# Block products for the attention's feature-major columns of the long sequence

## The chip, the cores and the metric

The kernel runs on one core of a Trainium2 chip. That core has five engines that run side by side, each with a queue of its own: TensorE (PE, matrix products; its weight loads are shown as PEld), VectorE (DVE), ScalarE (ACT), GpSimd (POOL) and SyncE (SP), which here issues nearly all DMAs. The metric is the time of one execution in microseconds of the device; lower is better.

## The reference

One layer of an encoder is computed for two inputs: a short sequence of 1024 tokens (s = 0) and a long one of 2048 tokens (s = 1), each with 16 learned meta tokens ahead of it. All numbers are fp32.

```python
xn = _rmsnorm(h, g_pre)
proj = xn @ w_in + b_in            # 1024 -> 6672 columns
na_q, na_k, na_v, na_z, ml_qk, ml_v, ml_z, ml_o, ml_g, mg = jnp.split(proj, SPLIT_IDX, axis=-1)
ya = (_neighbourhood_attention(na_q, na_k, na_v, na_rpb) * silu(na_z)) @ w_a
yb = (_mlstm_branch(ml_qk, ml_v, ml_g, ml_o, ml_conv_w, ml_head_g) * silu(ml_z)) @ w_b
ga, gb = split(sigmoid(mg), 2)
y = (ga * ya + gb * yb) @ w_out
return h + _rmsnorm(y, g_post)
```

The attention has 8 heads of 64 features; its queries see a window of 8 x 16 cells of a grid 64 cells wide, and the meta tokens. The mLSTM has 4 heads of 128 features, runs forwards and backwards in chunks, and passes a state from chunk to chunk.

## The kernel before, in words

*Exactness.* The products run on operands of the type F32R. Each fp32 operand is split into a high part and a low part, and each product is three matmuls: high x high, high x low, low x high (mm3, L197 to L202).

*Dense and sparse work.* Two Python generators are interleaved. `sparse` (L1990) is the mLSTM and the attention, in the order mLSTM short, attention short, mLSTM long, attention long. `dense` (L1943) is the large products: the input projection group by group, then the final groups (`final`: the branch projections with the merging by gates, then the output projection). After each sparse step `run` (L2008) takes dense work until its planned cost is used up. The planned cost of a step is `A_N[s]` for the attention (0.94 and 1.085 us), `A_A` and others for the mLSTM. One attention unit (`na`, L1019: one head, one row block of 512 queries, one of four column blocks) has four steps; the long sequence has 4 x 8 x 4 = 128 units and the short one 64. If a sparse stage needs a dense group that isn't done, dense work runs alone until it is. TensorE's instructions stay in the order that this interleaving writes; the other engines' order is set by a scheduler.

*Dense groups.* `PLAN` (L41) lists them as (sequence, first token, columns), each over 1024 tokens, that is two halves of 512. "m" are the mLSTM's columns, "n" the attention's (Q, K and Z feature-major, 12 columns of 128 features; V token-major), "g" the 16 columns of the gates. A feature-major column of a half is 8 depth tiles x 3 = 24 matmuls of 128x512 (`fm_half`, L666), and its result is evacuated by `fm_evac` (L616) from one of three PSUM banks into a staging tile "st" of four buffers and stored to DRAM.

*Block products.* The gates of the long sequence (`sgates`, L880) take the columns in pairs. A pair, the two halves of the tokens and the two halves of the depth make a 2 x 2 block product, which is computed with 7 products of 4 depth tiles instead of 8, from sums and differences of the operands. The weights' combinations are made once by `wprep` (L555) and kept in DRAM (tiles q...); the activations' combinations are made by `tprep` (L586) for each 1024 tokens, beside the group "n" of those tokens, stored, and loaded by `tload` into a pool that takes the place of the pool bp (`gopen`, `gclose`). Where a block group follows another with other tokens, its first two pairs ("lead") are computed in the plain way while the operands of the others are loaded. `beside` (L539) issues these preparations step by step, every few dense yields ("turns").

*Weights.* `requests` (L796) writes down all weight tiles in the order of use. `wpump` (L275) loads each ahead of use into four buffers; a tile seen for the first time is split into its parts, which are stored for later groups. A block unit is the high and low part of one product's weights, 512 KB.

*The attention's inputs.* `na_prep` (L1088) loads one head's raw queries (qr), keys (kr), values (vr) and Z (zt), and splits them into the tiles stk, qB, kd, kx and vt, in six pieces beside the units of the head before.

Of the kernel before, what the change touches and what calls it, by code (L numbers as in the profile page):

```python
# [2 lines left out]

# [6 lines left out]
F32 = mybir.dt.float32  # L10
# [7 lines left out]
P = 128  # L18
TCARGS = dict(schedule_with_timeline_sim=True)
D = 1024  # L20
# [20 lines left out]
PLAN = ((0, 0, "m"), (0, 0, "n"), (1, 0, "m"), (1, 1024, "m"), (1, 1024, "n"), (1, 0, "n"), (1, 0, "g"), (1, 1024, "g"), (0, 0, "g"), ("f", 0, 0), ("f", 0, 1), ("f", 1, 0), ("f", 1, 1), ("f", 1, 2), ("f", 1, 3))  # L41
SW = ((1, 0), (1, 1024))
OPS = ("11", "12", "21", "22", "s1", "s2", "s3", "s4")
# [8 lines left out]
FM_COLS = [c + P * j for c in (C_NQ, C_NK, C_NZ, C_MQ, C_MK, C_MZ) for j in range(4)] + [C_GA + P * j for j in range(16)]  # L52
TM_COLS = [(C_NV, 256), (C_NV + 256, 256), (C_MV, 256), (C_MV + 256, 256), (C_MO, WU), (C_MO + WU, WU)]
# [79 lines left out]
A_N, A_D, A_A, A_G = (0.94, 1.085), 1.63, 1.79, 1.3  # L133


class K:
# [3 lines left out]
    def __init__(self, tc, ins, outs):  # L140
# [10 lines left out]
        self.side, self.qd, self.TD = None, {}, {}  # L151
# [123 lines left out]
    def wpump(self, most=NBW, parts=1, copy=None):  # L275
# [4 lines left out]
        while self.wraw and self.wout < most:  # L280
# [14 lines left out]
            else:  # L295
# [7 lines left out]
                self.wkept[key] = []  # L303
                for x, part in ((hi, "h"), (lo, "l")):
# [152 lines left out]
    def build_half(self, s, t0, res):  # L457
# [14 lines left out]
        if s == 0:  # L472
# [23 lines left out]
            def rows():  # L496
# [4 lines left out]
                self.side, self.pace = self.wprep(), 4  # L501
# [37 lines left out]
    def beside(self):  # L539
# [5 lines left out]
        if self.side and self.turn % self.pace == 0:  # L545
            with self.behind():
                if next(self.side, "end") == "end":
                    self.side = None

    def drain(self):  # L550
        while self.side:
            if next(self.side, "end") == "end":
                self.side = None

    def wprep(self):  # L555
# [6 lines left out]
        for p in range(8):  # L562
            raw = pool.tile([P, 2, 2, 512], F32, name="pr", bufs=1)
            for f in range(2):
                nc.sync.dma_start(raw[:, f].rearrange("p a c -> p (a c)"), self.i["wu"][unit["i", C_GA + (2 * p + f) * P, P], :, :D])
            for _ in range(3):
                yield
            for f, ops in ((0, ("11", "12")), (1, ("21", "22")), (1, ("s3", "s1")), (0, ("s2", "s4"))):
# [14 lines left out]
                yield  # L583
                yield
# [81 lines left out]
    def fm_half(self, col, w, x, s, t0, meta, done=None, tags=None, late=None):  # L666
# [10 lines left out]
        for j, (q, k) in enumerate(order):  # L677
# [3 lines left out]
            wh, wl = (w[k % 2][:, 0, k // 2], w[k % 2][:, 1, k // 2]) if col >= C_GA else (w[0][:, k, :], w[1][:, k, :])  # L681
# [100 lines left out]
    def layout(self, cols):  # L782

        fm = dict(m=[c + P * j for c in (C_MQ, C_MZ, C_MK) for j in range(4)], n=[c + P * j for c in (C_NQ, C_NK, C_NZ) for j in range(4)],
                  g=[C_GA + P * j for j in range(16)])
        tm = dict(m=[(C_MO, WU), (C_MO + WU, WU), (C_MV, 256), (C_MV + 256, 256)],
                  n=[(C_NV, 256), (C_NV + 256, 256)], g=[])
# [4 lines left out]
    def lead(self, j):  # L792

        return [] if PLAN[j - 1][:2] == PLAN[j][:2] else [0, 1]

    def requests(self):  # L796
# [3 lines left out]
        for j, (s, t0, cols) in enumerate(PLAN):  # L800
# [3 lines left out]
            else:  # L804
                keys = []
                for kind, c in self.layout(cols):
                    if j >= 3 and ahead:
                        keys.append(ahead.popleft())
                    if cols == "g":
                        continue  # L810
                    keys += [("i", x, P) for x in c] if kind == "fm" else [("t", *c, a) for a in range(2)]
                if cols == "g":
                    assert not ahead
                    pairs = list(range(8))
# [65 lines left out]
    def sgates(self, s, t0, lead, nxt):  # L880
# [3 lines left out]
        for hf in range(2):  # L884
            if hf == 0:
                ws = [self.wtake(1)[0] for _ in range(2 * len(lead))]
            for u, w in enumerate(ws):
# [4 lines left out]
                yield from self.fm_half(C_GA + (2 * p + f) * P, w, self.xs[hf], s, t0 + 512 * hf, False, done=self.wdone if hf else None)  # L892
        for _ in more:
            pass
        pairs = [p for p in range(8) if p not in lead]
# [31 lines left out]
        for i, p in enumerate(pairs):  # L927
# [8 lines left out]
            out(2 * p, 0, new(), A)  # L936
# [6 lines left out]
            c22, c21 = new(), new()  # L943
            nc.vector.tensor_tensor(c22, E, u7, op=ALU.add)
# [7 lines left out]
            out(2 * p, 1, new(), E)  # L952
            A, E, R = R, A, E
        if nxt:
            self.xs = nx

    def group(self, s, t0, meta, cols, reuse, nxt):
# [3 lines left out]
        nb = None  # L961
        sw = (s, t0) in SW and cols == "n"
        if sw:
            self.drain()
            self.side, self.pace = self.tprep(s, t0), 3
            sw = (s, t0, "g") in PLAN[:PLAN.index((s, t0, "n")) + 2]
        for j, (kind, c) in enumerate(jobs):
# [6 lines left out]
            if last and sw:  # L974
                self.drain()
                self.gopen()
                for _ in self.tload(s, t0, (1, 2, 3)):
                    pass
            ws = self.wtake(len(c))
            for hf in range(2):  # L980
# [16 lines left out]
                for u, (col, w) in enumerate(zip(c, ws)):  # L997
                    for q, cost in enumerate(self.fm_half(col, w, self.xs[hf], *todo[hf], done=self.wdone if hf else None, tags=tags, late=late)):
# [89 lines left out]
    def na_prep(self, np_, s, rows, heads, j):  # L1088
# [6 lines left out]
        qr = np_.tile([P, 512], F32, name="qr", bufs=1)  # L1095
        stk = np_.tile([P, 4, P], F32R, name="stk", bufs=2)
        qb = self.qB[hh]
        nc.sync.dma_start(qr[0:64], self.NQ[s][pr][h0:h0 + 64, rt * 512:(rt + 1) * 512])
        sv = stk.rearrange("p b t -> p (b t)")
# [987 lines left out]
```

## Time and profile before

| | |
|---|---|
| median of the runs | 2732.97 us (2728.5 to 2733.58, 3 runs) |
| profiled execution, its own time | 2734.13 us |
| span in the profile | 2732.4 us |
| TensorE busy | 2691.8 us, 16144 matmuls |
| VectorE busy | 1877.1 us |
| ScalarE busy | 1389.1 us |
| moved by DMA | 762.76 MB |
| mean granted TensorE clock | 0.994 |

A row of a group gives the line, the engine, the operation, output <- inputs with tile shapes and a count; behind the bar the busy time and the mean of one in ns; behind the second bar the engine's idle time just before them, with what ended it. A row of the waits gives who waited <- for whom, the total in us, the number of times and the longest. A row in order of time gives the start and the length in us. A matmul's length overlaps the next one's. A row of a stretch gives its length, then busy time and count of each engine, the granted clock, the share of the DMA engines and GB/s.

### The profile page before, as it was taken

How to read it: one execution, taken by the hardware profiler on the slowest of the kernel's cores; microseconds unless marked ns; L12 is line 12 of the kernel's file. 1: busy time of each engine (PE TensorE's matmuls, PEld its weight loads, DVE VectorE, ACT ScalarE, POOL GpSimd, SP SyncE). 2: the span in 40 equal slices, each digit the busy share in tenths (PEclk: the TensorE clock that was granted, in tenths of full speed). 3: DMA queues.
4: the chain of work that ended last, by engine and by line, in shares of the span. 5: the costliest groups of instructions: out<-in, count | busy, mean ns of one | idle time of the engine just before them, and what ended most of it. 6: DMA issues, size and time to landing. Idle time of an engine off the chain costs nothing.

```text
span 2732.4 us, 47321 instructions
## 1 busy us (share of the span) xinstructions
PE 2691.8 (99%) x16144; PEld 2372.7 (87%) x16144; DVE 1877.1 (69%) x5174; ACT 1389.1 (51%) x3302; POOL 16.7 (1%) x100
## 2 busy tenths in 40 slices
PE   9999999999999999999999999999999999999998
PEld 7998897899789988788898888787888989989898
DVE  5443687876657765569877576573668798897844
ACT  6322556654456554456545564562455656555421
POOL 0000000000000000000000000000000000000000
PEclk9999999999999999999999999999999999999999
DMA  9987888986878755779888889989559898989975
GB/s 372 344 283 280 311 283 313 334 290 236 297 236 281 237 194 192 253 244 346 299 285 301 269 262 380 317 281 296 160 176 312 259 316 263 330 268 296 311 250 207
DMA packets 397538, 762.76 MB, mean 279 GB/s; under 512 B 50192, under 2 KB 179168, under 8 KB 395760
## 3 DMA queue, kind: packets, MB, share of 16 engines
q1 hardware_dynamic: 396176, 757.04, 81.9%
q0 software_dynamic: 1120, 2.69, 0.4%
q8 instruction: 128, 2.10, 0.3%
q14 instruction: 114, 0.93, 0.1%
HBM read 514.89 MB, written 244.69 MB: 278 GB/s over the span
## 4 chain that ended last, share of the span: by engine, by line
PE 87%; DMA 7%; DVE 3%; ACT 2%; issue 1%; SPq 0%; DVEq 0%; ACTq 0%
PE pj L200 14%; PE pj L202 13%; PE pj L201 13%; PE pj L720 5%; PE pj L722 5%; PE pj L721 5%; PE pj L1849 3%; PE pj L1848 3%; PE pj L1850 3%; PE pj L912 3%; PE pj L914 3%; PE pj L913 3%; PE sm L1197 3%; PE tr L1182 3%; DMA va<-mv 1%; DMA whi<-q 1%
## 5 line engine op out<-in xcount | busy, mean ns | idle before, releaser
L200 PE MATMUL pj<-xh,whi 128*128 128x512 f32 (+1 forms) x1376 | 539.3, 392 | 1.6 <-ACT whi L301 1.4
L202 PE MATMUL pj<-xh,wlo 128*128 128x512 f32 (+1 forms) x1376 | 525.4, 382 | 1.1 <-DMA wlo<-wl 0.8
L201 PE MATMUL pj<-xl,whi 128*128 128x512 f32 (+1 forms) x1376 | 525.5, 382 | 0.1
L720 PE MATMUL pj<-whi,xh 128*128 128x256 f32 (+1 forms) x1152 | 330.6, 287 | 0.0
L721 PE MATMUL pj<-wlo,xh 128*128 128x256 f32 (+1 forms) x1152 | 326.1, 283 | 0.0
L722 PE MATMUL pj<-whi,xl 128*128 128x256 f32 (+1 forms) x1152 | 326.1, 283 | 0.0
L202 PEld LDWEIGHTS pj<-xh,wlo 128*128 128x128 f32 x1376 | 259.7, 189 | 54.9 <-DMA wlo<-wl 1.2
L200 PEld LDWEIGHTS pj<-xh,whi 128*128 128x128 f32 x1376 | 260.0, 189 | 44.7 <-ACT whi L301 2.2
L201 PEld LDWEIGHTS pj<-xl,whi 128*128 128x128 f32 x1376 | 260.2, 189 | 41.3 <-issue 1.0
L720 PEld LDWEIGHTS pj<-whi,xh 128*128 128x128 f32 x1152 | 218.7, 190 | 0.4
L721 PEld LDWEIGHTS pj<-wlo,xh 128*128 128x128 f32 x1152 | 218.6, 190 | 0.1
L722 PEld LDWEIGHTS pj<-whi,xl 128*128 128x128 f32 x1152 | 218.4, 190 | 0.0
L1848 PE MATMUL pj<-whi,mh 128*128 128x256 f32 x768 | 216.3, 282 | 0.4 <-DMA whi<-wh 0.4
L1850 PE MATMUL pj<-whi,mlo 128*128 128x256 f32 x768 | 216.0, 281 | 0.0
L1849 PE MATMUL pj<-wlo,mh 128*128 128x256 f32 x768 | 215.9, 281 | 0.0
L1189 DVE TENSOR_TENSOR pts<-tr,pts 96x384 fp32r<-96x384 f32 (+2 forms) x192 | 119.0, 620 | 68.2 <-ACT pts L1184 66.1
L1184 ACT ACTIVATE pts<-tr 96x384 fp32r<-96x384 f32 (+2 forms) x192 | 103.6, 540 | 109.1 <-PE tr L1182 108.1
L200 PE MATMUL pj<-yh,whi 128*128 128x512 f32 x384 | 154.6, 403 | 0.0
L202 PE MATMUL pj<-yh,wlo 128*128 128x512 f32 x384 | 152.0, 396 | 0.0
L201 PE MATMUL pj<-yl,whi 128*128 128x512 f32 x384 | 151.3, 394 | 0.0
L1848 PEld LDWEIGHTS pj<-whi,mh 128*128 128x128 f32 x768 | 144.9, 189 | 1.7 <-DMA whi<-wh 0.6
L1849 PEld LDWEIGHTS pj<-wlo,mh 128*128 128x128 f32 x768 | 144.7, 188 | 1.0
(363 smaller groups left out, 6112.0 us busy)
## 6 DMA issues: line engine op xcount, KB each, us to landing
whi<-wh SPq DMA_DIRECT2D x160, 512.0 KB
wlo<-wl SPq DMA_DIRECT2D x160, 512.0 KB
wraw<-wu SPq DMA_DIRECT2D x48, 512.0 KB
wh<-whi SPq DMA_DIRECT2D x48, 512.0 KB
wl<-wlo SPq DMA_DIRECT2D x48, 512.0 KB
gt<-st SPq DMA_DIRECT2D x96, 256.0 KB
tg<-gt SPq DMA_DIRECT2D x96, 256.0 KB
whi<-q SPq DMA_DIRECT2D x45, 512.0 KB
```

Source lines behind the costliest of these rows:

```text
L200: mm(out, ah, bh, start=start, stop=False)
L201: mm(out, ah, bl, start=False, stop=False)
L202: mm(out, al, bh, start=False, stop=stop)
L720: nc.tensor.matmul(o, xh, wh, start=k == 0, stop=False)
L721: nc.tensor.matmul(o, xh, wl, start=False, stop=False)
L722: nc.tensor.matmul(o, xl, wh, start=False, stop=k == KT - 1)
L912: mm(bank, w[:, 0, k], xh[:, k], start=fresh and k == 0, stop=False, skip_group_check=True)
L1184: nc.scalar.activation(pts[:ks, :nb, 0, :], pt[:ks, :nb], AF.Copy)
L1189: self.nc.vector.tensor_tensor(pts[:ks, :nb, 1, :], pt[:ks, :nb], pts[:ks, :nb, 0, :].bitcast(F32), op=ALU.subtract)
L1848: nc.tensor.matmul(o, mh[:, k, xs], wh, start=clear > 0 and k == 0, stop=False)
L1849: nc.tensor.matmul(o, mh[:, k, xs], wl, start=False, stop=False)
L1850: nc.tensor.matmul(o, ml[:, k, xs], wh, start=False, stop=clear < 2 and k == KT - 1)
```

## The change

For the long sequence the 12 feature-major columns of the attention are computed as block products too. The groups "n" and "g" of the same 1024 tokens become one group "ng" of 14 pairs, and the attention's token-major V columns ("v") move into the mLSTM's groups. `nprep` makes the combined weights of the six new pairs; `wprep` goes on making those of the eight gate pairs. The four plain quarters of a new pair's weights are written when these weights are first split, in the short sequence's group. The activations' combinations are made beside the group "mv" of the tokens. In `sgates` the results go out through `fm_evac`. The pace constants of the attention change. In the attention's pool the raw queries are loaded into stk and the raw keys into kx, where their split parts end up as well, and Z has one buffer, loaded later; that is 8 KB per partition less.

```diff
-PLAN = (... (1, 1024, "m"), (1, 1024, "n"), (1, 0, "n"), (1, 0, "g"), (1, 1024, "g"), (0, 0, "g"), ...)
+PLAN = ((0, 0, "m"), (0, 0, "nv"), (1, 0, "mv"), (1, 1024, "mv"), (1, 1024, "ng"), (1, 0, "ng"), (0, 0, "g"), ...)
-A_N, A_D, A_A, A_G = (0.94, 1.085), 1.63, 1.79, 1.3
+A_N, A_D, A_A, A_G = (1.08, 0.965), 1.63, 1.79, 1.3
+N_COLS = FM_COLS[:12]
+PAIRS = [tuple(c[2 * p:2 * p + 2]) for c in (N_COLS, FM_COLS[24:]) for p in range(len(c) // 2)]
...
 def wpump
+                if key[1] in N_COLS and key[0] == "i":
+                    j = N_COLS.index(key[1])
+                    for a in range(2):
+                        d = self.qd[j // 2, f"{j % 2 + 1}{a + 1}"] = self.dp.tile([P, D], F32, name=f"q{j}{a}")
+                        for h, x in enumerate((hi, lo)):
+                            self.hold.append((d[:, 512 * h:512 * h + 512], x[:, 512 * a:512 * a + 512].bitcast(F32)))
...
-                self.side, self.pace = self.wprep(), 4
+                self.wside = self.wprep()
+                self.sides.append([self.wside, 3])
...
+    def nprep(self):
+        op = lambda o, a, b, x=ALU.subtract: nc.vector.tensor_tensor(o, a, b, op=x)
+        for p in range(6):
+            r0, r1 = [self.bp.tile([P, 2, 512], F32, name="xr", bufs=4) for _ in range(2)]
+            for f, r in enumerate((r0, r1)):
+                nc.sync.dma_start(r.rearrange("p a c -> p (a c)"), self.i["wu"][unit["i", PAIRS[p][f], P], :, :D])
+            for _ in range(2):
+                yield
+            op(r1[:, 1], r1[:, 0], r1[:, 1], ALU.add)
+            op(r1[:, 0], r0[:, 0], r1[:, 0])
+            yield
+            op(r0[:, 0], r1[:, 1], r0[:, 0])
+            op(r0[:, 1], r0[:, 1], r0[:, 0])
+            yield
+            for r, ops in ((r1, ("s3", "s1")), (r0, ("s2", "s4"))):
+                hi = self.bp.tile([P, 2, 512], F32, name="xr", bufs=4)
+                nc.scalar.activation(hi.bitcast(F32R), r, AF.Copy)
+                op(r.bitcast(F32R), r, hi)
+                for q, o in enumerate(ops):
+                    d = self.qd[p, o] = self.dp.tile([P, D], F32, name=f"q{p}{o}")
+                    nc.sync.dma_start(d[:, :512], hi[:, q])
+                    nc.sync.dma_start(d[:, 512:], r[:, q])
+                yield
...
 def sgates
-        def out(c, t, st, x):
-            bi = 36 + c
-            nc.scalar.activation(st, x, AF.Tanh, bias=self.bfh[:, bi:bi + 1], scale=0.5)
-            nc.sync.dma_start(self.GT[s][c][:, t0 + 512 * t:t0 + 512 * t + 512], st)
+        def out(f, t, x):
+            self.fm_evac(PAIRS[p][f], s, t0 + 512 * t, False, [(0, 512)], [x])
...
-            c22, c21 = new(), new()
+            c22 = new()
             nc.vector.tensor_tensor(c22, E, u7, op=ALU.add)
-            out(2 * p + 1, 1, c22, c22)
-            nc.vector.tensor_tensor(c21, A, u7, op=ALU.add)
-            out(2 * p + 1, 0, c21, c21)
+            out(1, 1, c22)
+            nc.vector.tensor_tensor(u7, A, u7, op=ALU.add)
+            out(1, 0, u7)
...
 def group
+        sw = (s, t0) in SW
         if sw:
-            self.drain()
-            self.side, self.pace = self.tprep(s, t0), 3
+            last = t0 > 0
+            self.sides.append([chain(self.tprep(s, t0), self.nprep() if last else ()), 2 if last else 4])
...
+            if last and sw and t0:
                 self.gopen()
-                for _ in self.tload(s, t0, (1, 2, 3)):
-                    pass
+                more = self.tload(s, t0, (1, 2, 3))
...
 def na_prep
-        qr = np_.tile([P, 512], F32, name="qr", bufs=1)
+        qr = sv.bitcast(F32)
-        kr = np_.tile([P, 16, 64], F32, name="kr", bufs=1)
+        kr = kx.bitcast(F32)
...
-            nc.scalar.activation(sv[0:64], qr[0:64], AF.Copy)
+            nc.scalar.activation(qb[0:64], stk[0:64].bitcast(F32), AF.Copy)
         yield
-        nc.scalar.activation(qb[0:64], stk[0:64].bitcast(F32), AF.Copy)
-        nc.vector.tensor_tensor(sv[64:128], qr[0:64], sv[0:64].bitcast(F32), op=ALU.subtract)
+        nc.vector.tensor_tensor(sv[64:128], qr[0:64], qb[0:64].rearrange("p b t -> p (b t)").bitcast(F32), op=ALU.subtract)
+        nc.scalar.activation(sv[0:64], qb[0:64].rearrange("p b t -> p (b t)").bitcast(F32), AF.Copy)
...
+        if hh:
+            zt = np_.tile([P, 512], F32, name="zt", bufs=1)
+            nc.sync.dma_start(zt, self.NZ[s][pr][:, rt * 512:(rt + 1) * 512])
```

More of the change, by code (lines that the diff above doesn't have):

```diff
@@ L2 @@
 from contextlib import ExitStack, contextmanager
+from itertools import chain
 import numpy as np
@@ L544, in beside @@
                 self.nc.sync.dma_start(*self.xput.popleft())
[L545 to L548, printed above, removed]
+        for x in tuple(self.sides):
+            if self.turn % x[1] == 0:
+                with self.behind():
+                    if next(x[0], "end") == "end":
+                        self.sides.remove(x)
     def drain(self):
-        while self.side:
-            if next(self.side, "end") == "end":
-                self.side = None
+        for x in self.sides:
+            for _ in x[0]:
+                pass
+        self.sides = []
     def wprep(self):
@@ L935, in sgates @@
             yield from prod(E, "s2", False)
-            out(2 * p, 0, new(), A)
+            out(0, 0, A)
             yield from prod(R, "s3", True)
@@ L951, in sgates @@
             yield from prod(E, "s4", False)
-            out(2 * p, 1, new(), E)
+            out(0, 1, E)
             A, E, R = R, A, E
+            if p == 5:
+                self.done.add(("n", s, t0))
         if nxt:
```

78 lines of the change are left out of this document (43 added, 35 removed).

## The prediction

> **What bounds the kernel now.** I read the page first, then the groups of instructions by shape, the waits of TensorE and the stretches.
>
> ```profile
> span 2732.4 us, 47321 instructions
> PE 2691.8 (99%) x16144; PEld 2372.7 (87%) x16144; DVE 1877.1 (69%) x5174; ACT 1389.1 (51%) x3302; POOL 16.7 (1%) x100
> DVE  5443687876657765569877576573668798897844
> q1 hardware_dynamic: 396176, 757.04, 81.9%
> PE 87%; DMA 7%; DVE 3%; ACT 2%; issue 1%; SPq 0%; DVEq 0%; ACTq 0%
> ```
>
> TensorE is busy in 99% of the span and makes 87% of the chain that ended last. VectorE reaches eight and nine tenths only in the last quarter. The DMA engines are 82% occupied, so they have no great reserve either. "Busy" can hide slow matmuls, so the next view is the order of time: two runs of back-to-back matmuls, first and last row of each. L200 to L202 are the plain products, L912 to L914 the block products.
>
> ```profile
> 1003.11 0.39 PE L200 MATMUL pj<-xh,whi 128*128 128x512 f32 x1
> ...
> 1004.26 0.39 PE L202 MATMUL pj<-xh,wlo 128*128 128x512 f32 x1
> 1525.44 0.40 PE L912 MATMUL pj<-t3h,wlo 128*128 128x512 f32 x1
> ...
> 1528.00 0.40 PE L914 MATMUL pj<-t3h,wlo 128*128 128x512 f32 x1
> ```
>
> Between the first pair lie 5 starts in 1.15 us, 0.230 us each; between the second 11 starts in 2.56 us, 0.233 us each. A row's 0.39 us overlaps its neighbours and is no price. A 512-wide matmul thus takes 0.231 us of TensorE in either form. Where TensorE does stand still, the waits and the stretches tell (columns of a stretch: length; busy time and count of PE, PEld, DVE, ACT, POOL; granted clock; DMA share; GB/s).
>
> ```profile
> PE tr L1469 <- DVE kf L1433: 6.1, 2, 4.3
> PE sc L1598 <- DVE nwy L160: 6.0, 1, 6.0
> PE pj L912 <- ACT pj L931: 1.3, 2, 0.8
> PE sm L1197 <- ACT prb L1165: 0.7, 2, 0.4
> 450.00:700.00 250.00, 247.14 (x1564) 222.42 (x1565) 186.95 (x590) 136.02 (x347) 0.90 (x8) 0.98 0.84 291
> 770.00:1085.00 315.00, 314.71 (x1992) 283.32 (x1991) 213.68 (x555) 174.34 (x381) 1.81 (x14) 1.00 0.70 231
> 1140.00:1200.00 60.00, 53.85 (x405) 52.41 (x404) 40.15 (x107) 25.74 (x73) 0.31 (x2) 0.91 0.87 284
> 1470.00:1855.00 385.00, 380.19 (x1895) 316.36 (x1894) 254.24 (x854) 216.66 (x574) 1.93 (x10) 1.00 0.92 306
> 1905.00:2600.00 695.00, 693.99 (x4298) 618.63 (x4298) 551.73 (x1366) 381.44 (x898) 2.04 (x4) 1.00 0.84 269
> ```
>
> These are the short sequence's mLSTM (its second half), its attention, the start of the long sequence's mLSTM, the block products of the gates beside that mLSTM, and the long sequence's attention. In the last TensorE loses 1 us of 695. So the time is the count of matmuls times their pitch, plus a few stalls.
>
> **The change part by part.**
>
> *Matmuls.* A pair of columns over 1024 tokens costs 2 columns x 2 halves x 8 depth tiles x 3 = 96 matmuls in the plain form, and 7 products x 4 x 3 = 84 as block products. Before, 16 gate pairs less the 2 that lead the second group, so 14, use the block form; after, 28 pairs less 2, so 26. That is 12 more pairs and 12 x 12 = 144 matmuls fewer, 16144 to 16000. At 0.231 us it is 33.3 us. All of it lies on the path, since TensorE has no idle time there to absorb it.
>
> A page of the Trainium skill ("TensorE: Matmul & The Clock Gate", section "Back-to-back issue gap") gives about 131 ns per matmul for a sustained stream of this width; by it the gain would be an estimated 18.9 us. The two runs above contradict it for these operands, and the sum goes by the runs.
>
> *Preparing the weights.* nprep forms the combined weights of six pairs, in work of this kind:
>
> ```profile
> L598 DVE TENSOR_TENSOR xr<-xh,xl 128x1024 f32<-128x1024 f32 x16 | 19.3, 1214 | 1.6 <-DMA va<-mv 1.5
> L600 DVE TENSOR_TENSOR xr<-xr 128x512 f32<-128x512 f32 x8 | 5.5, 686 | 0.6 <-DMA t2l<-xr 0.6
> L609 DVE TENSOR_TENSOR xr<-xr 128x1024 fp32r<-128x1024 f32 x8 | 9.8, 1222 | 13.2 <-ACT xr L608 13.1
> L608 ACT ACTIVATE xr<-xr 128x1024 fp32r<-128x1024 f32 x8 | 8.4, 1051 | 1.1 <-DVE xr L601 1.1
> L944 DVE TENSOR_TENSOR st<-pj,st 128x512 f32<-128x512 f32 x14 | 9.7, 690 | 7.9 <-PE pj L914 6.5 <-issue 1.4
> L938 ACT ACTIVATE pj<-pj 128x512 f32<-128x512 f32 x14 | 8.1, 581 | 8.7 <-PE pj L914 8.7
> ```
>
> Per pair: 4 x 0.686 + 2 x 1.222 = 5.2 us of VectorE and 2 x 1.051 = 2.1 us of ScalarE, so 31 and 13 us in all. It runs beside the short sequence's attention, where VectorE has 315 - 214 = 101 us free. There it meets the activation split of the second 1024 tokens, which moves too (tprep, four rounds of 2 x 1.214 + 6 x 0.686 + 1.222 = 7.8 us, 31 us), leaving some 40 us. The other split moves beside the mLSTM stretch 450 to 700, whose 63 us of free VectorE shrink to about 32. On TensorE this costs nothing while that cover lasts. Without it mLSTM steps wait as in the first two rows of waits: bounds 0 and the 6 us of one such wait per stretch; I take 2 us in all.
>
> *Evacuation.* Each further block pair needs 2 sums like L944 and 3 copies like L938: 12 x 2 x 0.69 = 17 us of VectorE and 12 x 3 x 0.58 = 21 us of ScalarE. Beside the mLSTM (385 us with 254 and 217 busy) both have room. What is on the path is a product waiting for its bank: 1.3 us over 14 pairs. The 12 more pairs give 1.1 us. The results now go through fm_evac, which takes a fresh staging buffer of four for each, and two for the Z columns. The fourth result of a Z pair can then find its buffer still being stored, with ScalarE queueing behind it and mLSTM steps behind ScalarE. No row shows this wait; its bounds are 0 and, for 4 Z pairs, 4 times the 4.3 us wait on kf, 17 us. I take 2 us, nearest to the bank waits. Evacuation: 3 us.
>
> *DMAs and queues.*
>
> ```profile
> DMA packets 397538, 762.76 MB, mean 279 GB/s; under 512 B 50192, under 2 KB 179168, under 8 KB 395760
> whi<-q SPq DMA_DIRECT2D x45, 512.0 KB
> xh<-xh SPq DMA_DIRECT2D x12, 1024.0 KB
> 1153.63 1.22 SPq L779 DMA_DIRECT2D nv<-stT  x2
> ```
>
> A block pair streams 3.5 MB of weights where a plain pair streams 2. By the order of the two programs, 84 more 512 KB loads of block operands and 48 fewer plain loads add 19 MB, nprep's loads and stores 19 MB. One fewer change of token group saves 8 loads of 1 MB and 32 stores of 256 KB, 17 MB. Net about 21 MB of 763, so 82% becomes about 85%. The block stage already ran at share 0.92, and the block products' largest wait there is the one on a bank, hence 0; without that cover the net 21 MB cost 21/763 of the span, 75 us, in waits. SP issues 80 more DMAs; at 0.6 us each that is 48 us spread over the span, ahead of weight loads that run four buffers ahead.
>
> *Moved work.* The V columns of the attention go into the earlier groups, and so do both splits. The long mLSTM's first head (1140 to 1200) therefore loses its neighbours: the V stores, 0.6 us of SP each, that stood ahead of its loads. That stretch lost 6.2 us to idling, and at clock 0.91 up to 5.4 us more to half rate. Block products now stand there, and they have waits of their own (4.8 us in 385). Bounds: minus 11.6 and 0; I take minus 5.
>
> *The attention's pool.* The raw query and key land in the tiles that hold the split operands, and the Z tile is single and loaded late. Instruction counts per head stay. The new wait is ScalarE's third copy behind VectorE's difference; queued behind it are the exponentials and the copies of transposed probabilities. Between them and TensorE stands a whole unit, 695/128 = 5.4 us. Bounds: 0, and the 0.4 us wait on prb once for each of 32 heads, 13 us; the value is taken with the next item.
>
> *Pace.* The planner's dense work per attention step falls from 1.085 to 0.965 us in the long sequence (128 units of 4 steps, 61 us less) and rises from 0.94 to 1.08 in the short (64 units, 36 us more). So the long attention packs into about 695 - 61 = 634 us. VectorE decides whether it can. Here are two stretches of gate merging, with attention beside and without, and the one VectorE row that counts the units:
>
> ```profile
> 2308.00:2364.00 56.00, 55.70 (x308) 47.60 (x308) 52.44 (x123) 27.95 (x61) 0.00 (x0) 1.00 1.05 342
> 2644.00:2688.00 44.00, 44.00 (x232) 37.59 (x231) 23.97 (x36) 4.90 (x9) 0.00 (x0) 1.00 0.96 353
> L1189 DVE TENSOR_TENSOR pts<-tr,pts 128x512 fp32r<-128x512 f32 (+1 forms) x10 | 6.3, 629 | 0.9 <-ACT pts L1184 0.8
> ```
>
> The 10 units in the first cost 52.4 - 24.0 = 28.5 us of VectorE, 2.85 each, and 56 - 44 = 12 us of TensorE, 1.2 each. By TensorE's order the five such stages hold 57 units after, where 50 stood, so 11.4 each: 24.0 + 11.4 x 2.85 = 56.5 us of VectorE against 44 + 11.4 x 1.2 = 57.7 of TensorE, 98% where 94% stood. VectorE idled 3.6 us in the first row; if it must idle as long again, a stage needs 60.1 us, 2.4 more than TensorE. The DMA share there is full already, but the bytes of a stage grow no faster than its length. Bounds for both items: 0, and 5 x 2.4 + 13 = 25 us. I take 5 us, one us a stage, nearest to the waits of 1 us that the stretch has now.
>
> *The sum.* 2734.1 (the profiled execution) - 33.3 + 2 + 3 - 5 + 5 = 2705.8 us. The median of the runs, 2733.0, is 1.1 us below the profiled one, so 2704.7, say 2705.
>
> **The rivals.**
>
> *Slower: the long attention can't run faster.* If VectorE, already at 94% beside gate merging, refuses the new pace, the attention keeps its 695 us, and the 61 us of dense work taken from its side come after it: 2705 - 5 + 61 = 2761. It decides from the point where about half of the shortening fails, 33 us of waits or 6.6 us in each merging stage. Against it: the sum of 98%, and the 1 us of TensorE waits in that stretch now. For it: a reserve of only 1.2 us per stage, and a new ScalarE wait behind VectorE's queue in each head.
>
> *Part of the gain goes in the block stage.* The staging-buffer wait at its bound (17 us rather than 2) and the attention's at its bound (25 rather than 5) would add 35 us and cancel the gain; half of that gives 2722. For it: DMA share 0.92. Against it: ScalarE is little more than half busy there.
>
> *No change.* The removed matmuls would be cover, and the waits of the mLSTM steps show instead. The 33 us would come back as idle time of TensorE, and the time stays at 2733. TensorE's 380 of 385 busy speaks against it.
>
> *More than the matmuls.* All 11.6 us of the first head's stall vanish and no new waits come: 2705 - 6.6 - 10 = 2688. In that row the clock falls with the stall. The Trainium skill's same page, section "Part 1: The HAM clock gate", says that about 3.4 us of idling halves TensorE's clock; this trace agrees (4.3 us of wait, then 0.91).
>
> **How the numbers follow.** Forecast (2695 to 2716) 0.58; more than the matmuls 0.13; part of the gain goes 0.15; no change 0.04; slower 0.10. A difference of 0.2%, 5.5 us, is about what runs of this kernel can tell from none. Faster 0.86, same 0.04, slower 0.10. The range reaches from the best case, 2688, to 2727, which leaves out the worse half of the partial loss and the slower rival.
>
> **What would show it.** PE count 16000 and busy about 2660 us; L912's successors 728 rows per line; VectorE near 1925 us, ScalarE near 1425; about 783 MB. The stretch of the first mLSTM head without kf waits and at clock 1.0. The long attention in about 634 us, merging stages with VectorE above 96% and TensorE waits under 2 us each. I am wrong if TensorE idles more than 15 us over the five merging stages, if ScalarE waits on stores of staging buffers, or if the attention's span stays near 695.

## The result, and the profile after

The changed kernel takes 2704.61 us (median of 4 runs, 2702.04 to 2705.33) against 2733.27 us before: a ratio of 0.9897, 95% interval 0.988 to 0.9914. It is faster by 1.0%; 2705 was forecast. The profiled execution took 2705.3 us with a span of 2703.3, 29.1 us less than the span before. From the page of the changed kernel:

```profile
span 2703.3 us, 47407 instructions
PE 2658.4 (98%) x16000; PEld 2345.6 (87%) x16000; DVE 1910.4 (71%) x5234; ACT 1418.5 (52%) x3350; POOL 17.4 (1%) x100
DMA packets 405986, 783.72 MB, mean 290 GB/s; under 512 B 51472, under 2 KB 180448, under 8 KB 404208
q1 hardware_dynamic: 404624, 778.01, 85.6%
```

TensorE has its 16000 instructions and 2658 us; VectorE grew by 33 us where 48 were counted, ScalarE by 29 where 34 were; the DMAs moved 21 MB more. The next rows are four of the six stages, of the kernel before and then of the changed one: the short mLSTM, the short attention, the long mLSTM and the long attention. Ahead of them lies the start, behind them the rest. The columns are the length, busy time and count of PE, PEld, DVE, ACT and POOL, the granted clock, the DMA share and GB/s.

```profile
267.00:765.00 498.00, 485.69 (x2973) 429.32 (x2972) 368.57 (x1075) 270.88 (x646) 6.74 (x34) 0.99 0.84 293
765.00:1081.00 316.00, 315.71 (x1996) 284.17 (x1995) 214.37 (x555) 175.23 (x381) 1.22 (x6) 1.00 0.70 229
1081.00:1899.00 818.00, 802.30 (x4300) 682.84 (x4299) 560.31 (x1783) 436.43 (x1140) 4.82 (x30) 0.99 0.87 294
1899.00:2604.00 705.00, 703.99 (x4359) 627.54 (x4358) 556.31 (x1378) 385.10 (x907) 2.04 (x4) 1.00 0.84 269
```

```profile
267.00:778.00 511.00, 494.46 (x3189) 445.71 (x3188) 391.76 (x1101) 269.71 (x641) 7.58 (x34) 0.98 0.88 305
778.00:1135.00 357.00, 352.24 (x2330) 320.66 (x2328) 272.32 (x655) 200.09 (x416) 1.23 (x6) 1.00 0.85 287
1135.00:1934.00 799.00, 796.20 (x3941) 663.05 (x3940) 524.02 (x1728) 450.02 (x1173) 4.64 (x30) 1.00 0.86 285
1934.00:2589.00 655.00, 647.88 (x4167) 583.94 (x4166) 541.73 (x1368) 377.89 (x904) 2.05 (x4) 1.00 0.87 276
```

Two things stand out. The long mLSTM idles 2.8 us where it idled 15.7, and the short mLSTM idles 16.5 where it idled 12.3. Idle time misses what half a clock costs, so for the comparison I use one number per stage, the *loss*: for each two neighbouring instructions of TensorE, the time from start to start less the median of that time for the same two shapes in the profile before, summed over the stage.

| loss in us | start | short mLSTM | short attention | long mLSTM | long attention | rest | sum |
|---|---|---|---|---|---|---|---|
| before | 8.0 | 24.5 | 9.8 | 31.5 | 12.7 | 1.2 | 87.8 |
| after | 9.9 | 35.0 | 11.9 | 10.5 | 21.1 | 2.4 | 90.8 |

Without loss the two orders differ by 32.3 us; with 3.0 us more loss, 29.3 are left, and the spans differ by 29.1. The sum of the losses hardly moved, but those of single stages did. Each loss is of one execution. How far it scatters shows in the long attention, whose code is the same in the changed kernel and in six of the variants below: there it lies between 17.5 and 21.4 us.

The five longest waits of TensorE in the changed kernel, and behind them that on the block product's bank:

```profile
PE sm L1247 <- ACT prb L1215: 4.7, 8, 1.3
PE sm L1200 <- DVE yg L1262: 4.5, 4, 2.1
PE sm L202 <- DVE num L1688: 4.4, 1, 4.4
PE sc L1648 <- DVE nwy L166: 4.3, 1, 4.3
PE sm L202 <- ACT kth L1522: 3.0, 1, 3.0
PE pj L955 <- ACT pj L972: 1.4, 2, 0.7
```

The first two are attention steps, the next three steps of the mLSTM, and the last is the bank: 1.4 us over 26 pairs, where 14 pairs had 1.3.

### The profile page after: what moved, and what is told of

Same layout as the page of the kernel before. It is cut to its first block, busy times and chain, and to the rows that moved or that the text cites. A ratio compares the mean times of both kernels' runs of the same rounds, so it can differ in the third digit from the quotient of the medians.

```text
span 2703.3 us, 47407 instructions
## 1 busy us (share of the span) xinstructions
PE 2658.4 (98%) x16000; PEld 2345.6 (87%) x16000; DVE 1910.4 (71%) x5234; ACT 1418.5 (52%) x3350; POOL 17.4 (1%) x100
## 3 DMA queue, kind: packets, MB, share of 16 engines
q1 hardware_dynamic: 404624, 778.01, 85.6%
## 4 chain that ended last, share of the span: by engine, by line
PE 70%; DVE 6%; DMA 5%; ACT 2%; issue 1%; SPq 0%; DVEq 0%; ACTq 0%
PE pj L202 8%; PE pj L203 8%; PE pj L204 8%; PE pj L955 6%; PE pj L957 6%; PE pj L956 6%; PE pj L1898 3%; PE pj L1899 3%; PE pj L1900 3%; PE pj L762 3%; PE pj L763 3%; PE pj L764 3%; PE sm L1247 2%; PE tr L1232 2%; DMA stk<-nq 1%
## 5 line engine op out<-in xcount | busy, mean ns | idle before, releaser
L202 PE MATMUL pj<-xh,whi 128*128 128x512 f32 (+1 forms) x992 | 385.5, 389 | 2.7 <-ACT st L679 1.5
L203 PE MATMUL pj<-xl,whi 128*128 128x512 f32 (+1 forms) x992 | 375.3, 378 | 0.1
L204 PE MATMUL pj<-xh,wlo 128*128 128x512 f32 (+1 forms) x992 | 374.7, 378 | 0.2 <-DVE wlo L304 0.2
L204 PEld LDWEIGHTS pj<-xh,wlo 128*128 128x128 f32 x992 | 188.0, 189 | 37.3 <-DVE wlo L304 0.4
L202 PEld LDWEIGHTS pj<-xh,whi 128*128 128x128 f32 x992 | 188.2, 190 | 33.8 <-ACT st L679 2.0
L203 PEld LDWEIGHTS pj<-xl,whi 128*128 128x128 f32 x992 | 188.4, 190 | 28.9 <-issue 1.0
L1900 PEld LDWEIGHTS pj<-whi,mlo 128*128 128x128 f32 x768 | 145.3, 189 | 0.0
```

The source lines that it names most:

```text
L202: mm(out, ah, bh, start=start, stop=False)
L203: mm(out, ah, bl, start=False, stop=False)
L204: mm(out, al, bh, start=False, stop=stop)
L1900: nc.tensor.matmul(o, ml[:, k, xs], wh, start=False, stop=clear < 2 and k == KT - 1)
```

## The experiments

### Is the gain the matmuls? (plain6)

The order, the pools, the pace and all preparation stay, but the six attention pairs of both groups go the plain way.

```diff
     def lead(self, j):
-        return c[:2] if PLAN[j - 1][:2] != PLAN[j][:2] else []
+        return [p for p in c if p < 6]
...
```

> The changed kernel with its order, its pools, its pace and all preparation kept, but with the six attention pairs of both token groups computed in the plain form: 16120 matmuls instead of 16000. If the gain is the matmuls at their pitch, the time rises by 120 x 0.231 = 27.7 us to about 2732, and it stands 24 x 0.231 = 5.5 us below the kernel before only if order, pools and pace together are neutral. If TensorE's work was cover for other waits, the time stays within 5 us of the changed kernel. If the order alone brought a part of the gain, it ends well below 2727.

Measured: 2729.02 us, 0.9991 of the kernel before (0.9979 to 1.0004). Its losses are 9.8, 35.8, 11.6, 10.8, 21.6 and 1.5: those of the changed kernel, stage by stage. Its span is 2732.1 us, 28.8 us more than the changed kernel's, for 120 matmuls; 120 times the pitch of 0.231 us are 27.7. That the two numbers are so close is partly luck, for the profiled execution took 4.8 us more than the median of this kernel. The medians of the two kernels are 24.4 us apart, or 25.7 when each is set against the kernel before in its own batch of runs (every batch repeated it). So a matmul is worth 0.20 to 0.24 us, which is the pitch as far as these runs can tell. Order, pools and pace together bring no gain: 24 matmuls fewer than before should bring 5.5 us, and about 2.7 came (by the interval, from 5.7 us faster to 1.1 slower).

### What relieved the long mLSTM? (b_v, b_t)

Two parts of the change, each put alone into the kernel before. First the V columns:

```diff
-PLAN = ((0, 0, "m"), (0, 0, "n"), (1, 0, "m"), (1, 1024, "m"), ...
+PLAN = ((0, 0, "m"), (0, 0, "nv"), (1, 0, "mv"), (1, 1024, "mv"), ...
-                  n=[(C_NV, 256), (C_NV + 256, 256)], g=[])
+                  n=[], v=[(C_NV, 256), (C_NV + 256, 256)], g=[])
...
```

> The kernel before with one part of the change: the attention's V columns computed in the mLSTM's groups, so that their stores don't stand beside the first head of the long mLSTM. Theory (SyncE's V stores delayed that head's loads): the waits of TensorE on kf and ktl there and the half clock vanish, 6 to 10 us, so 2723 to 2727. Rival (the activation split beside it, or the plain products, made the stall): 2733, give or take 2.

Measured: 2733.16 us, ratio 1.0004 (0.9995 to 1.0014), no change. The stretches of this kernel tell why: the first head of the long mLSTM, which stands later here than in the kernel before, and a stretch near the end.

```profile
1172.00:1225.00 53.00, 52.27 (x256) 42.72 (x255) 34.42 (x91) 31.74 (x90) 0.10 (x1) 1.00 0.77 257
2600.00:2660.00 60.00, 52.97 (x304) 45.86 (x303) 36.15 (x92) 17.45 (x48) 0.00 (x0) 0.94 0.57 195
```

In the first head TensorE idles 0.7 us instead of 6.2, at full clock, as the theory has it; the loss of the long mLSTM falls from 31.5 to 23.8. But dense work has moved ahead, at the old pace too little of it is left for the long attention, and the last merging stage waits 5.1 us for the attention's last rows. The rest after the attention loses 8.9 us instead of 1.2. That wait among TensorE's waits (sum, count, longest):

```profile
PE pj L200 <- ACT yh L1767: 5.1, 1, 5.1
```

The gain was given back.

Then the activation splits, in `group` of the kernel before:

```diff
+        if (s, t0) in SW and cols == "m":
+            self.side2, self.pace2 = self.tprep(s, t0), 2 if t0 else 4
         if sw:
-            self.drain()
-            self.side, self.pace = self.tprep(s, t0), 3
...
```

> The kernel before with one part of the change: both activation splits of the long sequence run beside the mLSTM groups of their tokens instead of the attention groups. TensorE's order is untouched. Theory (moving them trades a loss beside the short mLSTM for one beside the long): TensorE's loss in the short mLSTM grows from 24.5 to about 34 us and that in the long mLSTM falls from 31.5 by 8 us or more, so about 2733 in sum, give or take 4. Rival (the long mLSTM's relief comes from the order of the groups, not from these splits): the long mLSTM stays above 28 and the time rises to 2740 or more.

Measured: 2733.68 us, ratio 1.0008 (0.9998 to 1.0018). The loss in the short mLSTM grew from 24.5 to 34.1 us and that in the long fell from 31.5 to 23.1, as expected of the theory. Here are its stretches of the short mLSTM, of the long mLSTM, and of the first head of the latter:

```profile
267.00:775.00 508.00, 489.86 (x2980) 432.71 (x2978) 399.38 (x1117) 277.64 (x658) 6.43 (x34) 0.98 0.87 303
1092.00:1902.00 810.00, 799.45 (x4302) 680.33 (x4302) 520.30 (x1726) 422.02 (x1120) 4.85 (x30) 1.00 0.83 278
1142.00:1198.00 56.00, 52.99 (x437) 51.74 (x436) 33.35 (x100) 24.97 (x79) 0.10 (x1) 1.00 0.79 251
```

VectorE's busy time grew by 31 us in the one stage (368.57 before) and fell by 40 in the other (560.31 before); TensorE's loss grew by 10 us in the one and fell by 8 in the other. In the first head TensorE idles 3.0 us, at full clock, and its wait of 4.3 us on kf is gone, although the V stores still stand beside that head here. So moving the V columns and moving the splits each remove this wait: that the V stores alone made it is not shown, and the rival in the expectation for b_v is not excluded.

The V columns take 7.7 us from the long mLSTM and the splits 8.4, each alone. Since both remove the same wait, the two can't simply be added up towards the 21 us. The rest, around the switch from one block group to the next and the end of the stage, was not traced further.

### What does the short mLSTM pay for? (a_w4, a_tnone, a_tlate, a_tpool, a_tnodma, a_tfine)

The first suspect was the faster preparation of the gates' weights.

```diff
-                self.sides.append([self.wside, 3])
+                self.sides.append([self.wside, 4])
```

> The changed kernel with the gates' weight preparation issued every fourth turn, as before, instead of every third. The short mLSTM loses 10.5 us more to waits and half clock after the change than before it. Theory A (the faster preparation crowds VectorE ahead of the mLSTM's steps): those 10 us come back, 2694 to 2698. Theory B (the activation split that moved beside this stage, or the build of the next activations, is the cause): 2704, give or take 2.

Measured: 2712.46 us, ratio 0.9931 (0.9916 to 0.9946), slower than the change by some 8 us. The loss from 400 to 450 us did go (9.5 to under 2), but it came back at the other places, and what was left of the preparation was issued in one go ahead of the short attention, where 7.5 us were lost. So Theory A falls: a slower preparation moves a loss, but doesn't bring the 10 us back. Next the split itself was left out:

```diff
-            self.sides.append([chain(self.tprep(s, t0), self.nprep() if last else ()), 2 if last else 4])
+            self.sides.append([chain(self.tprep(s, t0), self.nprep()) if last else iter(()), 2 if last else 4])
         td = self.TD[s, t0]
+        self.TD[s, 0] = td
```

> The changed kernel without the activation split of the long sequence's first 1024 tokens (VectorE, ScalarE and stores left out); its block products read the split of the second 1024 tokens instead, so the attention columns and gates of those tokens are wrong. Theory B (this moved split, 31 us of VectorE, crowds the short mLSTM): the 7.3 us lost between 500 and 550 us fall to about 3 and those between 650 and 700 to under 1, 2697 to 2700. Rival (the stage's loss comes from the step that scales and splits the next activations, or from chance in the order): 2704, give or take 2. In no case should the 9.5 us lost between 400 and 450 us change, since the split starts later.

Measured: 2695.79 us, ratio 0.9864 (0.9845 to 0.9882). The loss in the short mLSTM is 24.6 us, what it was before the change; between 400 and 450 us it is 7.8, against 9.5 in the changed kernel. The stretch from 500 to 525 us, of the changed kernel and without the split:

```profile
500.00:525.00 25.00, 20.60 (x90) 16.94 (x89) 24.04 (x86) 11.32 (x28) 0.10 (x1) 0.86 0.63 215
```

```profile
500.00:525.00 25.00, 24.62 (x122) 20.26 (x121) 23.05 (x108) 17.70 (x43) 0.10 (x1) 1.00 1.01 347
```

VectorE had 24.0 of 25 us busy, TensorE stood idle for 4.4 and then ran at a lower clock. Without the split TensorE idles 0.4, though VectorE is still busy for 23.1 us; so the busy share by itself doesn't make the wait. The queue of VectorE just before (changed kernel, in order of time) shows what stood ahead of the step num that TensorE waited for:

```profile
504.65 0.68 DVE L641 TENSOR_TENSOR xr<-xr 128x512 f32<-128x512 f32 x1
505.26 0.88 DVE L1500 SCALAR_TENSOR_TENSOR vwl<-va,g_wT,vwh 128x130 fp32r<-128x130 f32 x3
506.05 0.42 DVE L1668 TENSOR_TENSOR sl<-um,sh 128x256 fp32r<-128x256 f32 x1
506.38 0.42 DVE L1483 SCALAR_TENSOR_TENSOR kf<-th,cv 128x256 f32<-128x256 f32 x1
506.72 1.22 DVE L535 TENSOR_TENSOR xl<-xt,xh 128x1024 fp32r<-128x1024 f32 x1
507.86 0.87 DVE L1766 BATCH_NORM_STATS2 bs<-hb 128x6 f32<-128x128 f32 x4
508.64 0.47 DVE L1688 TENSOR_TENSOR num<-sm,num 128x128 f32<-128x128 f32 x2
```

Of these rows L641 is the moved split. L535 splits the next activations, which both kernels do; the others are steps of the mLSTM. They follow each other without a gap. In the kernel without the moved split, num stands ahead of L535:

```profile
503.05 0.41 DVE L1484 SCALAR_TENSOR_TENSOR kf<-th,cv 128x256 f32<-128x256 f32 x1
503.38 0.28 DVE L1689 TENSOR_TENSOR num<-sm,num 128x128 f32<-128x128 f32 x1
503.58 1.21 DVE L535 TENSOR_TENSOR xl<-xt,xh 128x1024 fp32r<-128x1024 f32 x1
```

So the split costs more than its own time in this queue: with it, num also comes behind other work. What makes the scheduler put them in that order was not traced. Four ways to ease this were tried. A later start:

```diff
+        if t0 == 0:
+            for _ in range(16):
+                yield
...
-            ..., 2 if last else 4])
+            ..., 2 if last else 3])
```

> The changed kernel with the same split started 48 turns later and then issued every third turn instead of every fourth, so that part of it falls into the short attention, which is less sensitive. Theory B: 2 to 4 us less, 2700 to 2703, with the loss between 500 and 550 us reduced. Rival: 2704, give or take 2, with the loss moved to the place where the split now stands.

Measured: 2706.54 us, ratio 0.9897 (0.9874 to 0.992). The loss between 500 and 550 us went, and 5.5 us between 600 and 650 and 5.7 between 750 and 800 took its place: moved, not removed. The first of these holds a wait on VectorE (2.5 us on hb), the second a wait for a weight load, whose lateness was not traced:

```profile
PE pj L204 <- DMA wlo<-wl: 3.2, 1, 3.2
```

GpSimd for the sums and differences:

```diff
+        eng = nc.vector if t0 else nc.gpsimd
...
-                nc.vector.tensor_tensor(r, h[...], l[...], op=ALU.add)
+                eng.tensor_tensor(r, h[...], l[...], op=ALU.add)
...
```

> The changed kernel with the sums and differences of the first split (4 rounds of two wide and four narrow ones, 21 of its 31 us of VectorE) on GpSimd; the rest of it unchanged. Theory (VectorE's occupancy is what costs the short mLSTM its 10 us): two thirds come back, 2697 to 2699. Rival 1 (the split's DMAs or ScalarE are the cause): 2704, give or take 2. Rival 2 (GpSimd holds VectorE up while it works): 2704 or slower.

Measured: 2718.37 us, ratio 0.9948 (0.9932 to 0.9964): 14 us slower than the change. The loss in the short mLSTM is 48.7 us. The groups on GpSimd (busy time, mean ns of one):

```profile
L640 POOL TENSOR_TENSOR xr<-xh,xl 128x1024 f32<-128x1024 f32 x8 | 20.2, 2535 | 88.0 <-DVE xl L535 30.7 <-DVE st L1551 27.0 <-DVE den L1698 16.3
L642 POOL TENSOR_TENSOR xr<-xr 128x512 f32<-128x512 f32 x4 | 5.7, 1422 | 12.9 <-DVE den L1699 8.5 <-DMA t2l<-xr 3.1 <-DVE xl L535 1.2
```

Two of TensorE's three longest waits of that stage:

```profile
PE sm L204 <- DVE ktl L1524: 8.0, 1, 8.0
PE tr L203 <- DVE ccl L1641: 5.0, 1, 5.0
```

A sum takes 2.5 us there instead of 1.2, and VectorE's own busy time in the stage did not fall: 404 us in 525, where the change had 392 in 511. The order of time in this kernel shows why:

```profile
489.05 1.21 DVE L535 TENSOR_TENSOR xl<-xt,xh 128x1024 fp32r<-128x1024 f32 x1
490.34 2.40 POOL L640 TENSOR_TENSOR xr<-xh,xl 128x1024 f32<-128x1024 f32 x1 [29.53 <-DVE xl L535]
490.51 3.31 DVE L535 TENSOR_TENSOR xl<-xt,xh 128x1024 fp32r<-128x1024 f32 x1
641.21 5.01 POOL L640 TENSOR_TENSOR xr<-xh,xl 128x1024 f32<-128x1024 f32 x2 [13.58 <-DMA t0l<-xr]
643.86 2.39 DVE L162 TENSOR_SCALAR nwy<-nwy 128x4 int32<-128x4 int32 x1
```

L535 takes 1.21 us alone and 3.31 when it starts just behind a sum on GpSimd: it ends 1.1 us after that sum. L162, 0.17 us long in the changed kernel, takes 2.39 and ends with the second sum. The 36 VectorE instructions of this stage that overlap the split's work on GpSimd take 48.3 us; at the medians of the same instructions in the changed kernel they would take 17.6. These 31 us use up the 21 that were taken off VectorE, and more. So GpSimd holds VectorE up while it works, which was the second rival.

The split computed, but not stored:

```diff
+        if t0:
+            self.TD[s, 0] = td
...
-                        nc.sync.dma_start(d[:, e, :], ...)
+                        if t0:
+                            nc.sync.dma_start(d[:, e, :], ...)
```

> The changed kernel with the first split computed but its 32 stores of 256 KB left out; the block products of those tokens read the second split, so their columns are wrong. If the stores and SyncE's time for them are the cause, the time falls to about 2696 as without the whole split; if VectorE's work is, it stays at 2704, give or take 2.

Measured: 2702.06 us in the middle, with runs from 2696.76 to 2704.04, ratio 0.9892 (0.9874 to 0.991). The profiled run, the fastest of the four, lost 28.3 us in the short mLSTM, 6.7 less than the changed kernel; but between 500 and 550 us it lost 7.2, with the same wait of 4.4 us on num as with the stores. So the computing causes that one; what share of the remaining difference the stores have, these runs don't settle.

Smaller pieces:

```diff
-                nc.vector.tensor_tensor(r, h[:, ks, :512].bitcast(F32), l[:, ks, :512].bitcast(F32), op=ALU.add)
+                for v in range(2):
+                    nc.vector.tensor_tensor(r[:, v], h[:, 2 * e + v, :512].bitcast(F32), l[:, 2 * e + v, :512].bitcast(F32), op=ALU.add)
+                    if v or not t0:
+                        yield
...
```

> The changed kernel with the first split issued in smaller pieces: each sum of 128x1024 as two of 128x512, one sum or difference a step instead of two, a step every third turn instead of every fourth (44 steps x 3 = 132 turns instead of 28 x 4 = 112). The work is the same. Theory (an mLSTM step waits for the one wide block of VectorE work that stands ahead of it): the loss between 500 and 550 us falls from 7.3 to 3 or 4, 2699 to 2702. Rival (the sum of the occupancy counts, wherever it stands): 2704, give or take 2, with the loss moved.

Measured: 2707.0 us, ratio 0.9913 (0.9899 to 0.9926). That is 2 us more than the change, or 4 when each is set against the kernel before in its own batch, and above both expected ranges. The loss between 500 and 550 us is 6.9. Another 6.8 us appear between 750 and 800, again with a wait for a weight load:

```profile
500.00:525.00 25.00, 20.47 (x93) 16.69 (x93) 22.87 (x93) 9.27 (x22) 0.10 (x1) 0.93 0.78 257
PE sm L202 <- DVE num L1694: 4.5, 1, 4.5
PE pj L204 <- DMA wlo<-wl: 4.2, 1, 4.2
```

So the width of one piece is not what makes num wait. Nor is the sum of VectorE's occupancy shown to be it: here VectorE is busy for 22.9 of the 25 us and TensorE waits 4.5, without the split it is busy for 23.1 and TensorE waits 0.4.

### What does the long attention pay for? (b_napool, a_p90, a_p995)

The new pool can't be undone in the changed kernel, since the pool of the activation parts needs the space; so it was put alone into the kernel before, with `na_prep` as changed.

```diff
-        qr = np_.tile([P, 512], F32, name="qr", bufs=1)
+        qr = sv.bitcast(F32)
-        kr = np_.tile([P, 16, 64], F32, name="kr", bufs=1)
+        kr = kx.bitcast(F32)
...
```

> The kernel before with one other part: the attention's inputs landing in the split tiles, with the third copy on ScalarE behind VectorE's difference and one late Z tile. Theory: a unit of slack hides it, within 3 us of 2733. Rival: ScalarE's wait is passed on once a head, up to 0.4 us for each of 48 heads, 2740 to 2752, with TensorE waits on prb in both attention stages.

Measured: 2735.39 us, ratio 1.0013 (1.0003 to 1.0022), 1 to 6 us slower. The loss in the long attention is 16.1 instead of 12.7 us, and no other stage lost more. TensorE's named waits in that stage stay at this row:

```profile
PE sm L1198 <- ACT prb L1166: 0.6, 2, 0.3
```

So 3.4 us are lost in many gaps too small for the waits. That the pool makes them is not settled by one execution: b_v, with the old pool, has 15.8 there. The median lies within 3 us of 2733, as the theory said, though 3.7 above the kernel before in the same batch; the rival's 7 to 19 us did not come.

Then the pace, denser and looser:

```diff
-A_N, A_D, A_A, A_G = (1.08, 0.965), 1.63, 1.79, 1.3
+A_N, A_D, A_A, A_G = (1.08, 0.90), 1.63, 1.79, 1.3
```

> The changed kernel with 0.90 instead of 0.965 us of planned dense work per step of the long attention, so the attention packs into some 33 us less and the work left for the end grows by as much; TensorE's instructions are the same in number. Theory (VectorE is nearly full in the merging stages, so a denser attention makes TensorE wait): demand 24.0 + 12.1 x 2.85 = 58.5 us of VectorE against 44 + 12.1 x 1.2 = 58.5 of TensorE, full, so TensorE's loss in the attention grows from 21 to 30 or more, 2712 to 2720. Rival (the waits belong to single places such as the tiles' reuse, not to density): 2704 to 2707.

Measured: 2703.69 us, ratio 0.9891 (0.9872 to 0.991), no slower than the change. The attention lasts some 32 us less (its loss is 22.2 us), and as much more is left behind it. The density theory, as it was put, falls: the last step towards a full VectorE costs 1 us, not 9.

```diff
-A_N, A_D, A_A, A_G = (1.08, 0.965), 1.63, 1.79, 1.3
+A_N, A_D, A_A, A_G = (1.08, 0.995), 1.63, 1.79, 1.3
```

> The same with 0.995 us: 15 us more of dense work beside the attention. Density theory: the loss in the attention falls by 2 to 4 us, so 2701 to 2703, unless the last merging stage, which needs the attention's last rows, comes up before they are done; then the last units run without cover and the time rises to 2708 or more. Rival: no change, 2704 to 2706.

Measured: 2707.02 us, ratio 0.9905 (0.9887 to 0.9924). The loss in the attention is 18.1, 3 us less, as the density theory said, but within the scatter of 17.5 to 21.4; and the rest behind it loses 9.7 us. The last merging stage comes up before the attention's last rows, as this wait of the kernel shows:

```profile
PE pj L202 <- ACT yh L1816: 5.4, 1, 5.4
```

The loss of the five merging stages alone, each from its first merging instruction to its last, scatters less. It is 5.0 us before and 5.1 with the new pool at the old pace; 9.8 to 10.1 in the changed kernel and its six variants at 0.965; 10.1 at 0.995 and 11.9 at 0.90. So density costs something, about 5 us in all here, but there is no edge.

## Why the prediction was right, point by point

*Matmuls, 33.3 us.* Right: 32.3 us by the medians of the two orders, and 24 to 29 us for 120 of them alone (plain6). The 0.131 us per matmul that the Trainium skill gives (page "TensorE: Matmul & The Clock Gate", section "Back-to-back issue gap") would have made it an estimated 15.7 us for the 120; the rows for the pitch, and plain6, decide against it for these operands.

*Preparation, 2 us.* Undersized. The mechanism named (mLSTM steps behind VectorE's queue) is the one that happened, but 10.5 us were lost in the short mLSTM and 2.1 in the short attention. a_tnone shows that the first split alone makes the 10 us, and in b_t, the kernel before with both splits moved, the loss there grew by 9.6 us. The step that failed is the cover: 63 us free in 250 were taken for room, yet with the split in VectorE's queue one step, num, came 4.4 us late. How much of the 10 us is VectorE's work and how much the split's stores stays open (a_tnodma). Beside the mLSTM, each of whose steps waits for the one before, free time on average was no cover.

*Evacuation, 3 us, and moved work, minus 5.* Together minus 2 was expected of the long mLSTM and minus 21 came. The stall of its first head vanished as named. In the changed kernel this head stands at 1191 to 1242, and TensorE does not idle in it:

```profile
1191.00:1242.00 51.00, 51.00 (x254) 42.15 (x253) 29.64 (x85) 33.01 (x94) 0.10 (x1) 1.00 0.90 296
```

Its named cause, the V stores, is one of two parts of the change that each remove its longest wait (b_v, b_t). But the moved splits' relief was left out of the sum: they were charged where they went and not credited where they left, 8.4 us by b_t. The waits of the staging buffers, bounded at 17 us, did not reach TensorE, whose waits in this stage are the bank's 1.4 us of the row above and 1.4 us on a gate.

*DMAs, nothing.* Right: 21 MB more came, the queue is 85.6% occupied where about 85 were forecast, and TensorE's two waits on loads are 0.7 and 0.6 us.

*Pool and pace, 5 us.* Measured 8.4 us in the profiled execution, 4.8 to 8.7 over the scatter of the same code. About 5 of them are in the merging stages (5.0 before, 9.8 after): the one us a stage of the prediction. What goes beyond, up to 3.4 us, is outside them and had no share in the sum; it may be the pool's (b_napool). VectorE's 98% in the merging stages came nearly as forecast. Here are two of the changed kernel:

```profile
2134.00:2193.00 59.00, 58.72 (x322) 49.99 (x321) 57.47 (x138) 33.09 (x70) 0.00 (x0) 1.00 0.99 313
2256.00:2316.00 60.00, 58.73 (x320) 49.84 (x319) 58.00 (x141) 32.43 (x69) 0.00 (x0) 1.00 0.95 310
```

97% of VectorE, and TensorE idles 0.3 and 1.3 us; over the five such stages it idles 4.0, where more than 15 would have spoken against the forecast. That this is near an edge was wrong (a_p90), and with it falls the rival that the attention can't run faster: it ran 50 us shorter, where 61 were counted, and 32 us shorter again at 0.90.

*The sum.* 2705 against 2704.6 is partly luck. The matmul term was right. The terms beside it, plus 5 in sum, measured 3.0; single ones were off by 10.6 us (preparation, 12.6 with the short attention's share) and by 19 (moved work and evacuation), with opposite signs. In part these are two ends of the same move: in b_t the splits cost 9.6 us in the one stage and gave 8.4 in the other. The start and the rest, which had no term, lost 3.1 us more.

*The rivals.* "No change" is excluded by plain6. "Part of the gain goes" did not come: in the block stage no wait of TensorE goes back to the staging buffers, and the attention lost 8.4 us more and not 25. "More than the matmuls" had its mechanism: the first head's stall did go, and the gain was used up in the short mLSTM. A version without the cost of the first split would take about 2696 us (a_tnone); no way to get there was found among those tried, and none of the kernels run that compute the whole beats the change clearly.

## What to carry to other kernels

Where TensorE has no gaps, fewer matmuls are worth their pitch, and that can be counted in advance; measure the pitch from start to start and not from a row's length. Preparation that is moved must be charged where it goes and credited where it leaves, and both by the stage's sensitivity: a split with 31 us of VectorE, its copies and its stores cost 10 us beside a chain of dependent steps, whatever the average free time was. Look at what stands ahead of the waiting step in the queue, not only at the busy share: 24.0 of 25 us came with a wait of 4.4 us, 23.1 with one of 0.4. Stages with a queue of independent units (the attention) tolerated VectorE at 97% with losses of 1 to 4 us per stage.

## What was not expected of the hardware

VectorE at 97% over 60 us cost TensorE 0.3 to 1.9 us of idling per merging stage; a denser order cost no more. GpSimd took 2.5 us for a sum of 128x1024 where VectorE took 1.2. While GpSimd worked, VectorE's instructions stood with it: 36 of them took 48.3 us instead of 17.6, so with 21 us of work taken from it VectorE's busy time in the stage grew from 392 to 404 us.
